# Step sizes of a Mamba-2 layer as fp32 products on four groups of 32 output columns, C0 beside B0 in the opening of a hybrid decoder step

## The chip, the cores and the metric

The kernel is one launch on one core of a Trainium2 chip. Its metric is the time of one execution on the device in microseconds (us). A core has five engines that run their own instruction streams in order: TensorE (PE, matrix products into PSUM; its weight loads are listed as PEld), VectorE (DVE), ScalarE (ACT), GpSimd (POOL) and SyncE (SP), which here only issues transfers. SBUF is the working memory with 128 partitions; PSUM takes what PE writes, in eight banks of 512 fp32 columns.

## The reference, cut to what matters

One decoder layer for 1024 prompt tokens and 8 sample tokens that share all weights, so 1032 tokens in all. Every mixer reads the same RMSNorm(x) through one input projection `w_in`; one of them is a state space model whose step sizes `dt` come from 32 of its columns:

```python
sc_b, sc_c, sc_x, z, xbc, dt_raw, q, gates = jnp.split(xn @ w_in, splits, axis=-1)
xbc_c, ssm_conv_new = causal_depthwise_conv(xbc, ssm_hist, ssm_conv_w)
xbc_c = jax.nn.silu(xbc_c + ssm_conv_b)
xs, bm, cm = jnp.split(xbc_c, [SSM_D_INNER, SSM_D_INNER + SSM_GROUPS * SSM_STATE], axis=-1)
dt = jax.nn.softplus(dt_raw.astype(jnp.float32) + ssm_dt_bias.astype(jnp.float32))
a = -jnp.exp(ssm_a_log.astype(jnp.float32))
y_ssd, ssm_new = ssd_fn(xs, dt, a, bm, cm, ssm_s0)
```

`xbc` has 24 blocks of 128 columns: 16 of x, four of B, four of C. B0 and C0 are the first block of each (blocks 16 and 20). `z` has 16 blocks. A cross-attention reads keys and values made from RMSNorm of a memory of 256 tokens. All of it is fp32.

## The kernel before, in words

**Products.** Activations lie transposed: 8 tiles of 128 model columns by 1032 tokens. A large product is made of three passes in a faster format (fp32r): an operand is split into a high part (a cast by ScalarE) and the rest (a subtraction by VectorE), and high x high, high x low and low x high are summed in PSUM. A plain block of 128 output columns (`gemm`, L184) is 8 k-tiles x 3 passes x 3 thirds of 344 tokens = 72 matmuls; its PSUM tile has three banks, and two such tiles exist ("mm"). Two further banks ("sm", two buffers of one bank) serve all small products and transposes. Every weight block goes through `weights` (L146): a load of 512 KB, the cast, the subtraction; of raw, high and low tiles there are three each.

**The opening (L390 to L517).** x is loaded, normalised and transposed in three thirds. `to_xn` (L452) makes, for a third and a k-tile, `xw` (the normalised x in fp32, L458), its high part (L459) and its low part (L460), and writes the raw transpose to DRAM for later (L456, out of three buffers). `first_products` (L488) multiplies a third and k-tile by two weight blocks at once: dt's (128 columns of `w_in` of which the first 32 are dt) and B0's. The products of a third follow while the next third is made. Both "mm" tiles are taken by ps_dt and ps_B0. Behind the opening come the transposes of the histories for the convolutions (ps_h, L530), and ps_dt is emptied with its bias into dtr (L551).

**Behind the opening (L1151 to L1229).** `xbc_tile` (L735) takes B0 from PSUM (L739), convolves it (`conv`, L647: a scaled copy on ScalarE, three passes of 1.2 us on VectorE, small ones for the 8 sample tokens) and applies SiLU; two copies of a few columns on GpSimd keep the convolution's tail (L725) and B for the sample tokens (L732). C0 is a `gemm` of its own, then the same. `make_forms` (L1133) makes the sums and differences of the blocks of xn that the Strassen products need: with b11, b12, b21, b22 the quarters of xn (k-tiles 0 to 3 and 4 to 7, first and second half of the tokens), T1 = b12 - b11, T3 = b22 - b12, nT2 = T1 - b22 and T4, each in four k-tiles, in place in xw where that is possible, and each split into high and low. z0 and z1 are plain blocks (`z_step`, L757). From then on blocks go in pairs through `strassen` (L290), seven products of 24 matmuls (Z2 is the pair of z blocks 2 and 3; its weights are A, S, T and D, its forms B11, T1, nT2, B21, T3, B22, T4).

**Small pieces.** `pend` is a queue of small pieces of work which `tick` issues one at a time between the matmuls of a large product: three ticks in a plain block, three in a pair. Here it holds, in this order, the softplus of dt (`dt_softplus`, L562: nine transposes of dtr, then some twenty passes on VectorE), its running sums (`dt_sums`), their rows to DRAM (`dt_rows`) and what the sample tokens need (`dt_sample`: four copies into exs, L633, and 33 transposes into ps_ex). Then `flush` empties the queue, and the memory follows: its load, its norm (`mem_rms`, L1177), its transposes (`mem_t`) and 16 half blocks of keys and values (`kv_block`). The buffers of the dt work (pool "pdt") end at L1158, and the memory's (pool "pm", L1160) take their place.

**What sets the order.** A planner at compile time orders each engine's instructions: among those that it reckons ready, program order goes first; it also gives tiles their buffers. So work far behind can fill a gap, and an instruction whose buffer is still taken waits, with all that was put behind it on its engine. The buffers that matter most here are the five of the pool "ev" (4 KB a partition): x tiles, histories, dtr, the u and acc of a convolution, the raw differences for T3, z results, memory tiles and the sums of Strassen weights all rotate through them.

## Time and profile before

| what | value |
|---|---|
| median of 3 runs | 2502.28 us (2502.19 to 2504.86) |
| the profiled execution | 2503.04 us |
| its span in the profile | 2501.3 us |
| busy share of PE, DVE, ACT, POOL | 98%, 61%, 42%, 5% |
| granted clock of PE, mean | 0.995 |

The page is one execution taken by the hardware's profiler; times in it count from the span's start. Part 1 is the busy time of each engine, part 2 the span in 40 slices, part 4 the chain of work that ended last, followed back from the last instruction. In the order of time a row is: start, duration of one or length of the merged group, engine, line, operation, output <- inputs, shapes, xcount, and in brackets how long the engine was idle before it and what ended that. A matmul's row ends later than the next one starts, since they are pipelined; what a matmul takes is read from start to start. An fp32 matmul shows as two instructions. "128*32" is 128 rows by 32 columns of loaded weights.

### The profile page before, as it was taken

Reading aid. Unit: us, or ns where it says so; the run is one execution under the profiler, and the core shown is the slowest. Engines: PE = TensorE matmul, PEld = TensorE weight load, DVE = VectorE, ACT = ScalarE, POOL = GpSimd, SP = SyncE. Lnnn points to the kernel's source line nnn. Section 1 sums busy time; section 2 is a strip of 40 time slices with the busy share of each in tenths; the row PEclk is TensorE's granted clock in tenths of the full one; section 3 lists DMA queues with packets and bytes.
Section 4 is the critical chain, followed back from the end, with each engine's and each line's share of the span. In section 5 each row is a group of like instructions: output and inputs, shape, how many; then the busy total and the mean of one; then the engine's idle time right before and its main releaser. Section 6 shows DMA issues by size and latency. Waiting matters only on the chain.

```text
span 2501.3 us, 44971 instructions
## 1 busy us (share of the span) xinstructions
PE 2461.6 (98%) x18714; PEld 2399.9 (96%) x18714; DVE 1519.3 (61%) x2590; ACT 1047.0 (42%) x1688; POOL 135.3 (5%) x163
## 2 busy tenths in 40 slices
PE   7999999999999999999999999999999999999998
PEld 6999999999999998999989998999999999999998
DVE  6754586777677773766866662655775545453325
ACT  6554455454545534556545441223433333341212
POOL 0300000000000000321120000000000000000000
PEclk9999999999999999999999999999999999999999
DMA  6344434344344455668867686945442222282211
GB/s 202 110 150 154 128 104 143 110 140 126 99 136 136 127 160 190 192 211 266 276 199 277 218 303 218 327 144 178 140 151 95 85 68 85 86 274 89 68 34 69
DMA packets 348331, 392.08 MB, mean 157 GB/s; under 512 B 15334, under 2 KB 285782, under 8 KB 348119
## 3 DMA queue, kind: packets, MB, share of 16 engines
q1 hardware_dynamic: 327678, 331.50, 42.1%
q10 hardware_dynamic: 20449, 57.71, 6.1%
q8 instruction: 147, 2.41, 0.4%
q14 instruction: 57, 0.47, 0.1%
HBM read 280.40 MB, written 108.98 MB: 156 GB/s over the span
## 4 chain that ended last, share of the span: by engine, by line
PE 92%; DVE 2%; DMA 2%; ACT 2%; issue 1%; SPq 0%; ACTq 0%; DVEq 0%; POOL 0%
PE po L203 14%; PE pd L203 9%; PE ps_q L203 4%; PE pm L1701 4%; PE py L941 1%; PE pss L959 1%; PE ps_g L203 1%; PE po L933 1%; PE ps_z L203 1%; PE u20m L248 1%; PE u6m L248 1%; PE g20m L248 1%; PE u18m L248 1%; PE g18m L248 1%; PE u16m L248 1%
## 5 line engine op out<-in xcount | busy, mean ns | idle before, releaser
L1843 DVE TENSOR_TENSOR x<-pd,x 128x1032 f32<-128x1032 f32 x24 | 29.6, 1231 | 131.2 <-PE pd L203 131.2
L888 ACT ACTIVATE r<-r,acum 128x128 f32<-128x128 f32 x256 | 78.8, 391 | 5.3 <-DMA r<-ac_d 4.9
L659 DVE SCALAR_TENSOR_TENSOR ax<-u,prm,ax 128x1024 f32<-128x1024 f32 x44 | 56.3, 1280 | 0.1
L920 POOL TENSOR_TENSOR xdd<-xdt,decst 128x512 f32<-128x512 f32 x32 | 38.0, 1189 | 296.5 <-DVE xdt L916 296.5
L829 ACT ACTIVATE st<-st,es 128x128 f32<-128x128 f32 x128 | 41.9, 394 | 22.4 <-DMA st<-in_state_ssm_dram 20.5
L914 DVE TENSOR_TENSOR r<-r,cbm 128x1024 f32<-128x1024 f32 x32 | 39.0, 1218 | 9.5 <-ACT r L889 9.2
L1348 DVE TENSOR_TENSOR yr<-po,yr 128x1032 f32<-128x1032 f32 x8 | 9.9, 1232 | 53.8 <-PE po L203 53.8
L913 ACT COPY bT<-bp 128x128 f32<-128x128 f32 x32 | 8.5, 265 | 79.9 <-DVE cbm L911 79.9
L831 DVE SCALAR_TENSOR_TENSOR st<-sr,dts,st 128x128 f32<-128x128 f32 x128 | 40.2, 346 | 0.4
L941 PE MATMUL py<-r,xdt 128*64 128x128 f32 x512 | 35.9, 284 | 4.4 <-issue 4.4
L937 DVE TENSOR_TENSOR yt<-po,ea 128x512 f32<-128x512 f32 x28 | 19.3, 689 | 32.5 <-PE po L933 29.7
L941 PEld LDWEIGHTS py<-r,xdt 128*64 128x64 f32 x512 | 28.1, 139 | 8.7 <-issue 5.3
L950 DVE SCALAR_TENSOR_TENSOR x<-x,dpar,yt 128x128 f32<-128x128 f32 x128 | 36.2, 345 | 0.2
L835 DVE SCALAR_TENSOR_TENSOR sr<-st,sr 128x128 f32<-128x128 f32 x128 | 35.4, 286 | 1.1
L972 POOL TENSOR_TENSOR s<-s,cdec 128x512 f32<-128x512 f32 x28 | 35.1, 1253 | 0.5 <-DVE s L965 0.4
L889 ACT ACTIVATE r<-r 128x1024 f32<-128x1024 f32 x32 | 33.9, 1060 | 0.6
L959 PE MATMUL pss<-xdd,bT 128*128 128x512 f32 x64 | 33.5, 605 | 0.0
L1708 DVE TENSOR_TENSOR x<-pm,xT 128x516 f32<-128x516 f32 x16 | 11.1, 696 | 36.4 <-PE pm L1701 36.3
L933 PE MATMUL po<-bc,s 128*128 128x128 f32 x224 | 29.5, 275 | 0.0
L933 PEld LDWEIGHTS po<-bc,s 128*128 128x128 f32 x224 | 28.4, 191 | 0.0
L1630 DVE TENSOR_TENSOR gt<-po,gt 128x1032 f32<-128x1032 f32 x8 | 9.9, 1232 | 30.6 <-PE po L203 28.8
L662 DVE SCALAR_TENSOR_TENSOR ax<-u,prm,ax 128x1032 f32<-128x1032 f32 x22 | 28.3, 1286 | 0.0
(9105 smaller groups left out, 8947.7 us busy)
## 6 DMA issues: line engine op xcount, KB each, us to landing
r<-ac_d SPq DMA_DIRECT2D x32, 512.0 KB
gt<-gt_d SPq DMA_DIRECT2D x24, 516.0 KB
xs_d<-ax ACTq DMA_DIRECT2D x22, 516.0 KB
hr<-h_d SPq DMA_DIRECT2D x22, 516.0 KB
gt_d<-G ACTq DMA_DIRECT2D x20, 516.0 KB
x<-xs_d SPq DMA_DIRECT2D x16, 516.0 KB
zs<-zs_d SPq DMA_DIRECT2D x16, 516.0 KB
yb_d<-x SPq DMA_DIRECT2D x16, 516.0 KB
```

Of the source, the lines that this page charges most:

```text
L203: PE.matmul(ps[:, n, :CW], wt[:, ks], x[:, n * CW : (n + 1) * CW], start=(k == 0 and i == 0), stop=(k == nk - 1 and i == 2),)
L248: PE.matmul(ps[:, n, :HC], wt[:, ks], x[:, n * HC : (n + 1) * HC], start=(start and kt == 0 and i == 0), stop=(kt == 3 and i == 2), skip_g ...
L659: V.scalar_tensor_tensor(acc[:, :T], u[:, j : j + T], w[j], acc[:, :T], op0=ALU.mult, op1=ALU.add)
L829: S.activation(st[:, i], st[:, i], AF.Copy, scale=es[:, g * 4 + i, b : b + 1])
L831: V.scalar_tensor_tensor(st[:, i], rb, dts[:, g * 4 + i, b : b + 1], st[:, i], op0=ALU.mult, op1=ALU.add)
L888: S.activation(r[:, j, :], r[:, j, :], AF.Relu, scale=-1.0, bias=acum[:, c, h : h + 1])
L914: V.tensor_tensor(r, r, bc(cbm.unsqueeze(1), [P, HPG, P]), op=ALU.mult)
L920: G.tensor_tensor(b3(xdd, HPG), b3(xdt, HPG), bc(decst[:, c, hs].unsqueeze(2), [P, HPG, 64]), op=ALU.mult)
L933: PE.matmul(po[:, t * P : (t + 1) * P], state["s"][:, t * P : (t + 1) * P], bcg[1][:, cs], start=True, stop=True,)
L941: PE.matmul(py[hp : hp + 64, (h // 2) * P : (h // 2 + 1) * P], xdt[:, h * 64 : (h + 1) * 64], r[:, (h % 2) * 4 + h // 2, :], start=True, s ...
L959: PE.matmul(pss, bT, xdd, start=True, stop=True)
L1701: PE.matmul(ps[:, n, :HC], wt[:, ks], x[:, half * HT + n * HC : half * HT + (n + 1) * HC], start=(k == 0 and i == 0), stop=(k == KD - 1 an ...
```

## The change

- The two blocks of `first_products` are B0 and C0. Both "mm" tiles now hold these.
- dt's weight block is loaded but not split. After the products of a third, `step_sizes` multiplies it in plain fp32: 8 matmuls of 344 tokens, one per k-tile, with 32 loaded columns; k-tile k writes to the 32 partitions of group k mod 4, so that four groups hold a quarter of the sum each (two k-tiles). The result takes one "sm" buffer and goes by ScalarE, with the bias in the first group and 0 in the others, into dtr, which now has 128 partitions.
- `fold` (a sum of the four 32 x 32 blocks of the identity's rows) adds the four quarters: the nine transposes of dtr become nine fp32 products of dtr with fold, 32 columns each.
- xw is read by these products until the end of each third.
- C0's own `gemm` behind the opening is gone; `xbc_tile` takes B0 and C0 from PSUM one after the other, and both `make_forms` follow.
- The pieces of dt are ticked in z0 and z1. `mem_rms` writes its squares into PSUM (four activations of 512 columns and an addition in place of two of 1024) and keeps its sums in another pool, and it is ticked in z1; `flush`, the end of "pdt" and the start of "pm" come behind z1.

```diff
--- before.py
+++ after.py
@@ -393,7 +393,7 @@
     h_xc = cn.tile([P, 24, 24], F32, tag="h_xc", name="h_xc")
     xn = [(act_tile("ah", f"xnh{k}"), act_tile("al", f"xnl{k}")) for k in range(KD)]
     xw = [act_tile(("ah", "al")[k % 2], f"xw{k}", F32) for k in range(KD)]
-    ps_dt, ps_b0 = mm_ps("ps_dt"), mm_ps("ps_B0")
+    ps_b0, ps_c0 = mm_ps("ps_B0"), mm_ps("ps_C0")
 
     with tc.tile_pool(name="p0", bufs=1) as p0:
         xin = []
@@ -438,12 +438,17 @@
         def par(key, i):
             return prm[:, PC[key] + i : PC[key] + i + 1]
 
-        w_dt = weights(wblock(w_in, C_DT), "wdt")
         w_b0 = weights(wblock(w_in, C_XBC + 16 * P), "wB0")
+        w_c0 = weights(wblock(w_in, C_XBC + 20 * P), "wC0")
+        w_dt = load_raw(wblock(w_in, C_DT), "wdt")
+        bias = cn.tile([P, 1], F32, tag="bias", name="bias")
+        V.memset(bias, 0.0)
+        SY.dma_start(bias[:HEADS], a["ssm_dt_bias"].rearrange("l h -> h l"))
         st = p0.tile([P, 9], F32, tag="st", name="st")
         rst = p0.tile([P, 9], F32, tag="rst", name="rst")
         V.memset(st, 1.0)
         rbc = p0.tile([P, TT], F32, tag="rbc", name="rbc")
+        dtr = []
         xs_sb = p0.tile([NS, D], F32, tag="xs", name="xs_sb")
         for i in range(3, NCK):
             load_x(i)
@@ -489,10 +494,24 @@
             cw = slice(g3 * CW, (g3 + 1) * CW)
             ah, al = xn[k]
             ks = slice(k * P, (k + 1) * P)
-            for ps, (wh, wl) in ((ps_dt, w_dt), (ps_b0, w_b0)):
+            for ps, (wh, wl) in ((ps_b0, w_b0), (ps_c0, w_c0)):
                 PE.matmul(ps[:, g3, :CW], wh[:, ks], ah[:, cw], start=(k == 0), stop=False)
                 PE.matmul(ps[:, g3, :CW], wh[:, ks], al[:, cw], start=False, stop=False)
                 PE.matmul(ps[:, g3, :CW], wl[:, ks], ah[:, cw], start=False, stop=(k == KD - 1))
+
+        def step_sizes(g3):
+
+            cw = slice(g3 * CW, (g3 + 1) * CW)
+            ps = sm_ps(f"ps_dt{g3}")
+            for k in range(KD):
+                q = k % 4
+                PE.matmul(
+                    ps[q * HEADS : (q + 1) * HEADS, :CW], w_dt[:, k * P : k * P + HEADS], xw[k][:, cw],
+                    start=(k < 4), stop=(k >= 4),
+                )
+            if g3 == 0:
+                dtr.append(ev_tile("dtr"))
+            S.activation(dtr[0][:, cw], ps[:, :CW], AF.Identity, bias=bias)
 
 
         for i in range(3):
@@ -511,8 +530,11 @@
                     first_products(g3 - 1, k)
                 if g3 < 2 and k == 5:
                     root_of(g3 + 1)
+            if g3:
+                step_sizes(g3 - 1)
         for k in range(KD):
             first_products(2, k)
+        step_sizes(2)
 
         SY.dma_start(r_d, rbc[0:1, :])
 
@@ -545,10 +567,8 @@
 
     dt_stack = ExitStack()
     pd_ = dt_stack.enter_context(tc.tile_pool(name="pdt", bufs=1))
-    bias = pd_.tile([HEADS, 1], F32, tag="bias", name="bias")
-    SY.dma_start(bias, a["ssm_dt_bias"].rearrange("l h -> h l"))
-    dtr = ev_tile("dtr", (HEADS, TT))
-    V.tensor_scalar(t3(dtr), flat(ps_dt)[:HEADS], bias, None, op0=ALU.add)
+    fold = pd_.tile([P, HEADS], F32, tag="fold", name="fold")
+    V.tensor_reduce(fold, ident.rearrange("p (q h) -> p h q", q=4), axis=AX.X, op=ALU.add)
     W = 9 * HEADS
 
     def small(name):
@@ -562,8 +582,10 @@
     def dt_softplus():
         ps = sm_ps("ps_dtT")
         for c in range(NCK):
-            PE.transpose(ps[:, c * HEADS : (c + 1) * HEADS], dtr[:, c * P : (c + 1) * P], ident[:HEADS, :HEADS])
-        PE.transpose(ps[:NS, 256:288], dtr[:, T:TT], ident[:HEADS, :HEADS])
+            PE.matmul(
+                ps[:, c * HEADS : (c + 1) * HEADS], dtr[0][:, c * P : (c + 1) * P], fold, start=True, stop=True
+            )
+        PE.matmul(ps[:NS, 256:288], dtr[0][:, T:TT], fold, start=True, stop=True)
         V.memset(x0[:, 256:], 0.0)
         V.tensor_copy(x0[:, :256], ps[:, :256])
         V.tensor_copy(x0[:NS, 256:], ps[:NS, 256:288])
@@ -732,9 +754,7 @@
             G.tensor_copy(bcs[:, ct % 4, :, ct // 20], acc[:, T:TT])
         S.dma_start(xs_d[ct], acc[:, :TT])
 
-    def xbc_tile(ct, name, ps=None, w=None):
-        if ps is None:
-            ps = gemm(w, xn, "ps_" + name)
+    def xbc_tile(ct, name, ps):
         u = ev_tile("u" + name)
         S.copy(t3(u, 3), flat(ps))
         xbc_conv(ct, u, name)
@@ -1148,24 +1168,16 @@
             V.scalar_tensor_tensor(b12, b12, par("mix", kt), rb[:, HS[1]], op0=ALU.mult, op1=ALU.mult)
         return ts
 
-    w_c0 = weights(wblock(w_in, C_XBC + 20 * P), "wC0")
     xbc_tile(16, "B0", ps_b0)
+    xbc_tile(20, "C0", ps_c0)
     make_forms(0)
-    xbc_tile(20, "C0", w=w_c0)
     make_forms(2)
     z_step(0)
-    flush()
-    dt_stack.close()
-    mem_stack = ExitStack()
-    pm = mem_stack.enter_context(tc.tile_pool(name="pm", bufs=1))
-
-
-    mst = pm.tile([P, 2], F32, tag="mst", name="mst")
-    mrs = pm.tile([P, 2], F32, tag="mrs", name="mrs")
-    memT = [
-        (pm.tile([P, KD, P], F32R, tag=f"mh{m}", name=f"memh{m}"), pm.tile([P, KD, P], F32R, tag=f"ml{m}", name=f"meml{m}"))
-        for m in range(2)
-    ]
+
+
+    mst = cn.tile([P, 4], F32, tag="mst", name="mst")
+    mrs = cn.tile([P, 2], F32, tag="mrs", name="mrs")
+    memT = []
     mem_sb = []
 
     def mem_load():
@@ -1176,9 +1188,13 @@
 
     def mem_rms():
         for m in range(2):
-            junk = memT[m][0].rearrange("p k c -> p (k c)")
-            S.activation(junk, mem_sb[m], AF.Square, accum_out=mst[:, m : m + 1])
-        rsqrt(pm, mrs, mst, D, [P, 2], "m")
+            for half in range(2):
+                S.activation(
+                    sm_ps(f"junk{m}{half}"), mem_sb[m][:, half * 512 : (half + 1) * 512], AF.Square,
+                    accum_out=mst[:, 2 * half + m : 2 * half + m + 1],
+                )
+        V.tensor_add(mst[:, :2], mst[:, :2], mst[:, 2:])
+        rsqrt(cn, mrs, mst[:, :2], D, [P, 2], "m")
         for m in range(2):
             V.tensor_scalar(mem_sb[m], mem_sb[m], mrs[:, m : m + 1], None, op0=ALU.mult)
 
@@ -1223,10 +1239,16 @@
         S.dma_start(scr[:, :, c].rearrange("m p c -> p m c"), t)
 
     mem_load()
-    pend.extend([None, mem_rms, None])
+    pend.append(mem_rms)
+    z_step(1)
+    flush()
+    dt_stack.close()
+    mem_stack = ExitStack()
+    pm = mem_stack.enter_context(tc.tile_pool(name="pm", bufs=1))
+    for m in range(2):
+        memT.append(tuple(pm.tile([P, KD, P], F32R, tag=f"m{i}{m}", name=f"mem{i}{m}") for i in "hl"))
     pend.extend(lambda m=m: [mem_t(m, half) for half in range(2)] for m in range(2))
     pend.extend(lambda j=j, q=q: kv_block(j, q) for j in range(8) for q in range(2))
-    z_step(1)
 
     def plain3():
         for kt in range(4):
```

## The prediction

> **What bounds the kernel now.** I read the page first (busy shares and the chain of waits), then the busy time by stage, then the opening engine by engine.
>
> ```profile
> span 2501.3 us, 44971 instructions
> PE 2461.6 (98%) x18714; PEld 2399.9 (96%) x18714; DVE 1519.3 (61%) x2590; ACT 1047.0 (42%) x1688; POOL 135.3 (5%) x163
> PE 92%; DVE 2%; DMA 2%; ACT 2%; issue 1%; SPq 0%; ACTq 0%; DVEq 0%; POOL 0%
> ```
>
> TensorE (PE) is busy 98% of the span and is 92% of the chain that ended last. So a microsecond taken off PE counts only where PE then has something else ready, and the stage that changes has to be looked at by itself. The busy time by stage, up to the start of the memory keys (first number behind the comma: length of the stretch):
>
> ```profile
> core 0: us, PE busy (x) PEld busy (x) DVE busy (x) ACT busy (x) POOL busy (x), PEclk, DMA share, GB/s
> 57.40:61.71 4.31, 2.20 (x33) 2.04 (x33) 3.56 (x7) 4.28 (x7) 0.10 (x1) 1.00 0.14 24
> 61.71:75.52 13.81, 13.81 (x81) 13.53 (x82) 13.81 (x27) 7.71 (x10) 13.13 (x3) 0.88 0.20 71
> 75.52:100.35 24.83, 24.32 (x155) 23.62 (x153) 22.53 (x41) 16.24 (x21) 10.82 (x2) 1.00 0.31 109
> ...
> 105.94:125.62 19.68, 19.68 (x161) 18.88 (x160) 12.05 (x20) 9.32 (x13) 0.00 (x0) 0.94 0.35 92
> 125.62:140.84 15.22, 14.19 (x114) 13.74 (x113) 11.17 (x27) 14.56 (x37) 0.00 (x0) 0.97 0.39 139
> ```
>
> The stretches are: the seam behind the opening; C0's product; z0 and z1; Z2 from the first product of its form T1 on; Z4 up to the memory keys. The reader is to see two things. PE is full from 61.71 on. And VectorE (DVE) is as full: all of 13.81 us under C0, 22.53 of 24.83 us under z0 and z1. Only from 105.94 on has it room (12.05 of 19.68). The two engines arrive at Z2 together. The seam and C0 in order of time on PE:
>
> ```profile
> 57.31 2.29 PE L530 MATMUL ps_h<-ident,hist 24*128 24x24 f32 x32
> ...
> 61.71 1.23 PE L203 MATMUL ps_C<-xnh,wC0h 128*128 128x344 f32 x3 [2.11 <-DVE dtr L551]
> ...
> 65.23 0.63 PE L203 MATMUL ps_C<-xnl,wC0h 128*128 128x344 f32 x3
> ...
> 66.27 0.68 PE L565 MATMUL ps_dtT<-ident,dtr 32*128 32x32 f32 x8
> 66.91 0.74 PE L203 MATMUL ps_C<-xnh,wC0h 128*128 128x344 f32 x3
> ...
> 75.52 0.64 PE L203 MATMUL ps_z<-xnh,wz0h 128*128 128x344 f32 x3
> 75.99 0.63 PE L203 MATMUL ps_z<-xnl,wz0h 128*128 128x344 f32 x3
> ```
>
> C0 starts 2.11 us late because its PSUM buffer is the one that VectorE is still emptying into dtr. Its first 12 products (four rows of three) need 65.23 - 61.71 = 3.52 us; at z0's pace (three in 0.47 us, the last two rows) they would need 1.88, so a slow clock costs 1.6 us (granted 0.88 in the third stretch). C0 ends at 75.52.
>
> **The change, part by part.**
>
> *PE, products.* In the opening dt's 72 products of 344 columns give way to 72 of C0: equal. Behind it C0's own 72 go: 72 x 0.157 = 11.3 us less. The 24 fp32 products come on top. The trace has two neighbours: fp32 products on 32 columns in four groups (the cached values), and one fp32 product over the full array (ac).
>
> ```profile
> 1499.41 1.07 PE L1492 MATMUL pso<-vc,pTs 128*32 128x256 f32 x16
> 1500.41 0.74 PE L203 MATMUL po<-b03h,wo21h 128*128 128x344 f32 x3
> 96.94 0.59 PE L592 MATMUL ps_ac<-da,tri 128*128 128x256 f32 x2
> 97.37 0.59 PE L593 MATMUL ps_ac<-da,ones 128*128 128x256 f32 x2
> ```
>
> One fp32 product is two instructions. Over the full array, 256 columns take 97.37 - 96.94 = 0.43 us. Eight on four groups, 256 columns each, take 1500.41 - 1499.41 = 1.00 us, where one after the other they would take 3.44. So the groups overlap. Scaled by 344/256: 1.34 us for a third of the tokens, 4.0 for three. The upper bound is no overlap at all: 24 x 0.43 x 344/256 = 13.9 us. The lower is 24 products over four groups without any start cost, 3.5 us. I take 4.0, because that row has the same form (eight in a row, four groups, fp32 on both sides).
>
> The Trainium skill, "TensorEngine Tiling (Array Packing)", section "Theoretical Speedup", gives up to 4x for 32 columns, and its "Key Properties" say that a change of tiling mode drains the array. By the 4x the three thirds would be an estimated 3.5 us; the trace agrees with most of it (3.44 to 1.00 is 3.4x), and 1.00 less 2 x 0.43 leaves at most 0.14 us for entering and leaving the mode, so the drain does not change the sum.
>
> *The fold.* Nine transposes (66.27 to 66.91, 0.64 us) become nine fp32 products against fold, 18 instructions that each load 128 columns. Nearest row, fp32 with 128 loaded columns and a single moving one:
>
> ```profile
> 1056.21 2.06 PE L1060 MATMUL psny<-ones,sqa 128*128 128x1 f32 x18
> 1058.14 0.72 PE L203 MATMUL ps_q<-xnl,wq4h 128*128 128x344 f32 x3
> ```
>
> 18 in 1.93 us: +1.3 us. Bounds: 0.64 (as the transposes, +0) and 3.9 (18 at 0.21, half of the 0.43 above).
>
> *The seam.* With C0's product in the opening, z0 is the next large product. Its PSUM buffer is B0's, which ScalarE empties in 1.00 us (row below) while PE does the last third of the step sizes (1.34) and the history transposes (2.29). So the 2.1 us wait goes, and I let the 1.6 us of slow clock go with it, since PE no longer pauses there; if it stays slow, that is 1.6 back.
>
> Sum on PE: -11.3 + 4.0 + 1.3 - 2.1 - 1.6 = **-9.7 us**, if nothing new holds PE.
>
> *VectorE and ScalarE.* These rows of the groups and of the order of time carry it:
>
> ```profile
> L551 DVE TENSOR_SCALAR dtr<-ps_dt,bias 32x1032 f32<-32x1032 f32 x1 | 1.3, 1271 | 0.0
> L153 DVE TENSOR_TENSOR wz0l<-wz0r,wz0h 128x1024 fp32r<-128x1024 f32 x1 | 1.2, 1215 | 0.0
> 45.10 0.69 DVE L1127 TENSOR_TENSOR xw<-xw 128x516 f32<-128x516 f32 x1
> ...
> 51.60 0.69 DVE L1127 TENSOR_TENSOR xw<-xw 128x516 f32<-128x516 f32 x1
> 61.28 1.00 ACT L739 COPY uB<-ps_B 128x1032 f32<-128x1032 f32 x1
> 101.29 0.67 DVE L316 TENSOR_TENSOR Z2sa<-Z2sa,Z2r 128x512 f32<-128x512 f32 x1
> 105.41 1.23 DVE L236 TENSOR_TENSOR Z2Sl<-Z2sa,Z2Sh 128x1024 fp32r<-128x1024 f32 x1 [1.59 <-ACT Z2Sh L235]
> 117.33 0.67 DVE L633 COPY exs<-dtT 8x1024 f32<-8x1024 f32 x1
> 122.97 1.06 ACT L1180 ACTIVATE memh<-mem 128x1024 fp32r<-128x1024 f32 x1 [2.69 <-PE ps_ex L638]
> 128.52 1.42 DVE L1183 TENSOR_SCALAR mem<-mem,mrs 128x1024 f32<-128x1024 f32 x2
> ```
>
> dtr leaves VectorE (-1.27); ScalarE takes it in three pieces with room to spare (7.71 of 13.81 busy). One split of weights goes (wdt is used raw); as a third pair of split buffers is now free during the opening, z0's split can run there: -1.2 behind it. The reduction into fold is one small pass (0.2, as the other 128-column passes). In return the four differences b12 - b11 (45.10 to 51.60, 0.6 each) overwrite xw, which the step sizes now read: they must wait for the products of their third and move from the opening to its end, into the idle 2 us that VectorE has there (3.56 of 4.31 in the seam is mostly other work, so I count them as +1 of their 2.4). mem_rms no longer writes into the memory tiles, so it need not wait for the step-size buffers (2.69 us at 122.97, released by the last ps_ex): its 1.4 us of VectorE and some small steps, and perhaps dt_sample's 2.7 (four copies like that at 117.33), can come ahead of Z2.
>
> VectorE's backlog ahead of Z2 ended at 101.97 before. Now: 101.97 - 1.27 - 1.2 + 0.2 + 1 = 100.7, or 104.8 with memory and sample work put ahead. Z2's second factor needs a cast and a subtraction more (1.0 + 1.2): **T1's product can start between 102.9 and 107, against 105.94 before.** PE would be there at 105.94 - 9.7 = 96.2. So most of PE's gain turns into a wait for VectorE. I take 103.5, nearer the lower end, since the squares and the sample's copies hang on transfers that land late: 2.4 us gained there. What was done ahead need not be done again: of PE's hold-ups between 105.94 and 140.84 (idle 15.22 - 14.19 = 1.0 us, clock 0.94 of 19.68 us and 0.97 of 15.22 us, together 1.6) I take 2 of the 2.6. But PE's new wait of up to 7 us is longer than the 2.11 us that cost 1.6 us of slow clock at 61.71; products without a form (A's with B11 and B21) break it up, so I take half, 0.8 lost, with 0 and 1.6 as bounds. Together -2.4 - 2.0 + 0.8 = **-3.6 us**.
>
> The Trainium skill, "TensorE: Matmul & The Clock Gate", section "HAM oscillation — how this bites in real kernels", says that a gap of over some 3.4 us brings the slow clock back. The row at 61.71 shows it after 2.11 us of idleness behind 2.29 us of small transposes. By the rule the full 1.6 us would be lost and the sum would be an estimated -2.8 us.
>
> *Queues.* The third weight block stands ahead of the five x loads on SP's queue, and the tiles' write-back waits behind those:
>
> ```profile
> 7.75 0.58 SPq L124 DMA_DIRECT2D wB0r<-in_w_in_dram  x1
> 8.38 3.06 SPq L403 DMA_DIRECT2D x<-in_x_prompt_dram  x5
> GB/s 0 151 418 423 66 73 317 317 383 404 412 412 372 117 254 127 127 6 277 34 285 37 282 158 279 246 235 319 319 108 172 110 136 225 269 95 0 7 4 84
> 20.55 1.00 ACT L455 COPY xt<-ps_xt 128x384 f32<-128x384 f32 x2 [0.69 <-DMA xT_d<-xt]
> ```
>
> ScalarE waits there for the write-back (xT_d) until 20.55. The last row is what all transfers moved in the first 62 us, in slices of 1.55 us; 512 KB at its best slices of some 420 GB/s is 1.3 us more, at the mean of about 200 twice that. It is made up by the split of C0 that leaves the middle of the opening, so I count 0, bound +2.6. bias, 0.1 KB, likewise. mem_rms's two squares of 1.06 become four of 512 columns on ScalarE, which waits there anyway; mst and mrs only change pool. Order: step_sizes takes one of two small PSUM buffers that the transposes of x rotate through; bound three times an evacuation, +1.5 us, hidden if PE lags there as it does.
>
> **Rivals.**
>
> *A. VectorE does not bind* and PE keeps its gain: 2502.3 - 9.7 = 2492.6; with up to 2 us of small new waits I say 2493.5. For it: PE could fill the wait with sums that are ready. Against: the stretches above, 36.3 of 38.6 us busy.
>
> *B. GpSimd's small copies hold the evacuation buffers.* There are five ("ev"). B0 and C0 now stand together: two u, two acc, and a raw difference fill them, and the next to ask (the second raw difference, then z0's result) waits until a copy of 8 or 11 columns on GpSimd is done:
>
> ```profile
> 62.34 9.50 POOL L725 COPY tail_xc<-uB 128x11 f32<-128x11 f32 x1 [4.15 <-ACT uB L739]
> ...
> 76.80 0.23 POOL L725 COPY tail_xc<-uC 128x11 f32<-128x11 f32 x1 [1.33 <-ACT uC L739]
> 86.72 10.60 POOL L732 COPY bcs<-aC 128x8 f32<-128x8 f32 x1 [9.69 <-ACT aC L728]
> 97.34 0.34 SPq L1174 DMA_DIRECT2D mem<-in_mem_prompt_dram  x1
> ```
>
> The same copy takes 0.23 us at 76.80, where VectorE is idle, and 9.50 or 10.60 where it is full; SP's load of mem went out at 97.34, when the last one let go. If z0 or the raw difference waits out one such copy, that is up to 10.6 us less the forecast's 3.6: 2509.3, **slower**. It decides from a hold of over 5 us on; against it stands that VectorE itself waiting opens the gap in which the copy ends.
>
> The Trainium skill, "SBUF — State Buffer", section "SBUF: two separate sides", calls the port pair of VectorE and GpSimd an exclusive lock that the loser waits out; the 9.50 and 0.23 agree, and by it nothing bounds the hold while VectorE runs without a gap.
>
> *C. The groups do not overlap* with 344 moving columns: 13.9 instead of 4.0 puts PE at Z2 at 96.2 + 9.9 = 106, where it stood: 2501, with the little that is gained behind it. Against: the 1.00 us row.
>
> *D. The change does less than it says*: the planner fills the wait otherwise, or later stages move by as much. 2502.
>
> **How the numbers follow.** The profiled execution took 2503.04 us, 1.74 around its span; the median is 0.76 below it. The sum moves the median: 2502.3 - 3.6 = 2498.7. Chances: forecast 0.47, A 0.24, B 0.17, C 0.04, D 0.08. The forecast's own range is 2495.5 to 2501.5 (T1's product at 102 to 105, 0 to 2.6 us gained behind it). For 8 in 10 I go from 2491.5 (A with its best) to 2506 (two thirds of B). 0.2% is 5.0 us, about what a measurement of this kernel tells from none: the border is 2497.3, inside the forecast's own range; I put 0.16 of its 0.47 below it. Faster: 0.16 + 0.23 of A = 0.39. Slower: 0.16 of B and 0.02 of C and D = 0.18. Same: the remaining 0.43.
>
> **What would show it.** The step sizes: eight fp32 products on 128*32 in 1.2 to 1.5 us per third; 4.6 speaks for C. The seam: z0 directly behind the history transposes, without 2.1 us of idle PE. The wait: PE idle ahead of Z2S's products, released by VectorE; without it, A. GpSimd: a copy of over 5 us whose end releases a tile that PE or VectorE waits for, B. mem_rms on ScalarE ahead of Z2's end, and no wait on ps_ex there. I am wrong if PE reaches Z4 (125.62 before) earlier by less than 1 us or by more than 8, or if stages behind 141 move by over 2 us of their own.

## The result, and the profile after

The changed kernel took **2516.21 us** (median of 4 runs, 2513.40 to 2519.30), the kernel before 2502.24 (2500.27 to 2504.86) beside it: a ratio of 1.0052, 95% interval 1.0040 to 1.0064, so 14 us **slower**. The forecast was 2498.7. The profiled run of the changed kernel is the longest of its four, 2519.30 us; 3.1 us of what its trace shows at the end are above the median.

The page's first lines:

```profile
span 2517.6 us, 44946 instructions
...
PE 2464.4 (98%) x18699; PEld 2397.8 (95%) x18699; DVE 1519.2 (60%) x2591; ACT 1048.2 (42%) x1694; POOL 124.6 (5%) x163
...
PE 88%; DMA 4%; DVE 3%; ACT 2%; issue 1%; SPq 0%; ACTq 0%; POOL 0%; DVEq 0%
```

PE has 2.8 us more to do than before (2461.6), though 72 products of 0.157 us gave way to 24 others; its share of the chain that ended last fell from 92 to 88%. The busy time by stage, for the stretches that answer to those of before (the seam; z0 and z1; Z2 from T1's product on; Z4 up to the memory keys):

```profile
64.85:69.00 4.15, 3.28 (x43) 3.02 (x39) 3.49 (x9) 4.04 (x6) 0.32 (x3) 0.97 0.64 174
69.00:95.84 26.84, 25.72 (x157) 25.34 (x157) 25.31 (x42) 15.69 (x23) 12.34 (x3) 0.94 0.44 140
100.27:123.83 23.56, 18.51 (x147) 17.39 (x145) 15.85 (x31) 15.37 (x20) 0.00 (x0) 0.99 0.34 98
123.83:154.47 30.64, 23.93 (x169) 21.98 (x169) 16.92 (x37) 17.58 (x47) 0.00 (x0) 0.83 0.17 55
```

z0 starts at 69.00, where C0's product still ran before. Up to there PE gained 6.5 us (75.52 before). But in Z2 PE is idle for 5.05 of 23.56 us, and up to the keys for 6.7 of 30.64, at a clock of 0.83. PE in order of time:

```profile
63.55 1.36 PE L508 MATMUL ps_dt<-xw,wdtr 128*32 128x344 f32 x16
...
67.05 1.17 PE L552 MATMUL ps_h<-ident,hist 24*128 24x24 f32 x16 [0.42 <-ACT dtr L514]
68.18 1.00 PE L585 MATMUL ps_dtT<-fold,dtr 128*128 128x32 f32 x6
69.00 1.21 PE L203 MATMUL ps_z<-xnh,wz0h 128*128 128x344 f32 x3
...
73.34 1.19 PE L585 MATMUL ps_dtT<-fold,dtr 128*128 128x32 f32 x10
...
95.84 0.51 PE L248 MATMUL Z2m<-xnh,Z2Ah 128*128 128x258 f32 x2 [1.12 <-ACT z L780]
...
123.83 0.80 PE L248 MATMUL Z4m<-xnh,Z4Ah 128*128 128x258 f32 x2 [4.23 <-ACT Z4Ah L235]
...
150.21 1.59 PE L1206 MATMUL ps_mt<-ident,mem 128*128 128x128 f32 x8 [2.56 <-DVE meml L1211]
154.47 0.58 PE L1230 MATMUL ps_kv<-wkv00h,memh 128*128 128x256 f32 x1 [2.67 <-DVE meml L1211]
```

From Z2's first product (95.84, 100.35 before) to Z6's (173.5, 161.10 before) both kernels do nearly the same work on PE (after the change also ps_ac and one set of ps_acT, some 1.1 us, which stood ahead of Z2 before). The last row of the same view taken over that stretch, first before, then after (length of the stretch, PE busy, granted clock):

```profile
100.35:161.10 60.75, 59.72 (x485) 0.97 0.46 142
```

```profile
95.84:173.50 77.66, 65.79 (x493) 0.91 0.33 102
```

This is the whole loss: 4.5 us ahead at Z2, 16.9 us lost on the way, 12.4 us behind at Z6 and 12.8 to 14.1 us behind at each pair from there to 765. Idle PE makes 10.8 of it (11.87 against 1.03); the other 6.1 are busy time: that 1.1, and for most of the rest the slower clock (0.91 against 0.97). (A further 4.7 us come at X12 and G12, where ScalarE waits 8.3 us for loads of the sample state, 2.5 before. Whether they belong to the change isn't settled: in the two runs below with the memory part as before the same wait is 4.2 and 7.9 us, and the loss there 1.0 and 2.6.) So what comes late? VectorE's softplus of the step sizes, first before, then after, from the read of ps_dtT to its end in da (after with the pass just ahead):

```profile
71.70 0.41 DVE L568 COPY x<-ps_dtT 128x256 f32<-128x256 f32 x1
...
78.53 0.31 DVE L573 TENSOR_SCALAR z<-u 128x288 f32<-128x288 f32 x1 [1.57 <-ACT u L572]
...
95.60 0.46 DVE L585 SCALAR_TENSOR_TENSOR da<-dtT,abc 128x288 f32<-128x288 f32 x1
```

```profile
89.02 1.29 DVE L355 TENSOR_TENSOR T42al<-xw,T42ah 128x516 fp32r<-128x516 f32 x2
90.23 0.41 DVE L590 COPY x<-ps_dtT 128x256 f32<-128x256 f32 x1
...
97.58 0.31 DVE L595 TENSOR_SCALAR z<-u 128x288 f32<-128x288 f32 x1 [3.23 <-ACT u L594]
...
112.12 0.45 DVE L607 SCALAR_TENSOR_TENSOR da<-dtT,abc 128x288 f32<-128x288 f32 x1
```

ps_dtT lay ready at 74.6, yet VectorE reads it at 90.23: both convolutions and both sets of forms now stand ahead of it in program order, and VectorE works through these first, from 68 us on without a gap (the first row of the second view is one of their passes). Before, C0's product came between the two halves of that work, and the softplus was ticked in it. From there the delay runs on through ScalarE:

```profile
94.76 1.03 ACT L780 ACTIVATE z<-ps_z 128x1032 f32<-128x1032 f32 x1 [4.65 <-PE ps_z L203]
95.81 1.28 ACT L594 ACT_TABLE_LOAD   x1
...
97.10 0.45 ACT L594 ACTIVATE u<-u 128x288 f32<-128x288 f32 x1
...
112.89 1.28 ACT L645 ACT_TABLE_LOAD   x1
...
114.43 1.28 ACT L795 ACT_TABLE_LOAD   x1
...
116.95 1.28 ACT L620 ACT_TABLE_LOAD   x1
...
120.95 1.28 ACT L798 ACT_TABLE_LOAD   x1
...
122.74 1.04 ACT L235 CAST Z4Ah<-Z4r 128x1024 fp32r<-128x1024 f32 x1
...
129.79 0.59 ACT L318 COPY Z<-Z4m 128x516 f32<-128x516 f32 x1 [5.07 <-PE Z4m L248]
130.28 0.61 ACT L1192 ACTIVATE junk<-mem 128x512 f32<-128x512 f32 x1
```

The exponential stands behind z1's SiLU (which waits for PE until 94.76), with a table load of its own. What depends on da then falls into Z2's end, between the SiLUs of Z2: four table loads of 1.28 us within 10 us (before, Z2 has two in all up to that cast, at 100.31 and 114.00), and Z4Ah's cast, which PE waits for (4.23 us), comes at 122.74. The Trainium skill, "ScalarE: Activation LUTs", section "What ACT_TABLE_LOAD costs", gives 1.28 us for the load and 1.38 for a drain with it; the load agrees, and no drain shows here (95.81 to 97.10). The memory comes last: its squares stand on ScalarE behind Z4's first copy, which waits 5.07 us for the late PE, and are done only at 139, so its transposes and its keys slip as well (2.56 and 2.67 us of idle PE, and keys 13.6 us later than the 140.84 of before).

### The profile page after: what moved, and what is told of

Read it like the earlier page. It is cut to its first block, busy times and chain, and to the rows that moved or that the text cites. A ratio compares the mean times of both kernels' runs of the same rounds, so it can differ in the third digit from the quotient of the medians.

```text
span 2517.6 us, 44946 instructions
## 1 busy us (share of the span) xinstructions
PE 2464.4 (98%) x18699; PEld 2397.8 (95%) x18699; DVE 1519.2 (60%) x2591; ACT 1048.2 (42%) x1694; POOL 124.6 (5%) x163
## 4 chain that ended last, share of the span: by engine, by line
PE 88%; DMA 4%; DVE 3%; ACT 2%; issue 1%; SPq 0%; ACTq 0%; POOL 0%; DVEq 0%
PE po L203 12%; PE pd L203 9%; PE pm L1723 4%; PE ps_q L203 3%; PE ps_g L203 2%; PE py L961 1%; PE pss L979 1%; PE ps_z L203 1%; PE Z4m L248 1%; PE po L953 1%; PE C6m L248 1%; PE u20m L248 1%; PE g18m L248 1%; PE g14m L248 1%; PE g20m L248 1%
## 5 line engine op out<-in xcount | busy, mean ns | idle before, releaser
L957 DVE TENSOR_TENSOR yt<-po,ea 128x512 f32<-128x512 f32 x28 | 19.3, 689 | 32.8 <-PE po L953 32.8
L1730 DVE TENSOR_TENSOR x<-pm,xT 128x516 f32<-128x516 f32 x16 | 11.1, 695 | 36.4 <-PE pm L1723 36.3
L678 ACT ACTIVATE ax<-u,prm 128x1024 f32<-128x1024 f32 x22 | 27.4, 1246 | 2.3 <-DVE u L344 1.3
```

## The experiments

All were timed beside the kernel before, whose medians were 2503.5 to 2504.2 there; the times in bold are medians, and the ratios, taken over all runs, differ a little from those of the medians. The theory T at the start: the chain of the step sizes comes late, and all else with it. Rivals: the memory's rearrangement (R1), and the opening (R2).

### The order of the step sizes

```diff
-    pend.extend([None, dt_softplus, dt_sums, dt_rows, dt_sample])
...
-    xbc_tile(20, "C0", ps_c0)
     make_forms(0)
+    dt_softplus()
+    dt_sums()
+    xbc_tile(20, "C0", ps_c0)
     make_forms(2)
+    pend.extend([dt_rows, dt_sample])
     z_step(0)
```

> The kernel after, with the softplus and the sums of the step sizes put in program order between the forms of B0 and the convolution of C0, not behind both forms. Theory T (the chain of the step sizes comes late on VectorE and ScalarE, so its buffers come free late and the memory's transposes and keys with them): ps_dtT is read within 8 us of 74.6 in place of 90.2, da ends near 97 in place of 112.1, the memory's transposes start within 2 us of 130 in place of 145.9, ps_kv before 143 in place of 154.5, and the time falls by 10 to 16 us, to 2497 to 2506. Rival R1 (the memory part, squared into PSUM and flushed only behind z1, is what comes late by itself): the chain is early, ps_kv still starts behind 150, the time stays above 2510. Rival R2 (the opening, with three weight blocks ahead of most of x): ps_kv comes earlier but the time falls by less than 6 us.

**2507.08 us** (its runs spread from 2502.6 to 2512.2, and the profiled one took 2502.7), ratio 1.0012 (1.0004 to 1.0020): 9 us of the 14 are back. ps_dtT is read at 76.19, da starts at 96.03, the memory's transposes start at 127.2 (earlier than expected) and the keys at 137.4, 3.5 us ahead of before. T holds for the larger part (it had said 10 to 16 us); R1 as the cause of that part, and R2, fall. The edit also puts the first forms ahead of C0's convolution, and what that gives by itself isn't separated; the next run moves the softplus alone. But 3.5 us are still lost by the medians, and of PE's waits between 60 and 175 us this is the longest (total, times, longest):

```profile
PE Z4m L248 <- ACT Z4Ah L235: 4.5, 1, 4.5
```

The reverse, in the kernel before: only the queue's filling is moved.

```diff
-    pend.extend([None, dt_softplus, dt_sums, dt_rows, dt_sample])
...
     make_forms(2)
+    pend.extend([None, dt_softplus, dt_sums, dt_rows, dt_sample])
     z_step(0)
```

> The kernel before, and in it only the queue of the step sizes' pieces filled behind the forms of B0 and C0 in place of ahead of the convolutions, so that the softplus runs in z0 and not in C0's gemm. T: the same delay without anything else of the change: the read of ps_dtT near 90 in place of 71.7, ps_kv 8 to 14 us later than 140.8, the time 2510 to 2516. R1 and R2: within 3 us of 2502.

**2507.64 us**, 1.0015 (1.0006 to 1.0024): the delay alone, without the rest of the change, costs 4 us. T had said 8 to 14. The read came at 86.52 and the keys 6.3 us late, half of what they are in the change. The delay is a cause by itself; its price depends on what else is behind.

### The memory part

```diff
     z_step(0)
+    flush()
+    dt_stack.close()
...
-            for half in range(2):
-                S.activation(
-                    sm_ps(f"junk{m}{half}"), mem_sb[m][:, half * 512 : (half + 1) * 512], AF.Square,
...
+            junk = memT[m][0].rearrange("p k c -> p (k c)")
+            S.activation(junk, mem_sb[m], AF.Square, accum_out=mst[:, m : m + 1])
```

> The kernel after, with the memory part as it stood before: the pieces flushed and the step sizes' buffers closed behind z0, the memory's squares written into its own buffer. R1: ps_kv back near 141 to 145 and the time at or under 2506. T: the chain of the step sizes is still behind both forms (ps_dtT read near 90), so ps_kv stays behind 150 and the time within 4 us of 2516.

**2516.26 us**, 1.0053 (1.0041 to 1.0066), ps_dtT read at 90.51, the keys at 153.6: R1 falls. The same edit on top of the early step sizes:

> The kernel after with both undone: the softplus and sums of the step sizes between the forms of B0 and C0's convolution, and the memory part as before. What is left of the change is the arithmetic and the place of C0. Theory T2 (with the step sizes early, the memory's squares are the next to hold ScalarE, in four pieces that wait for the small PSUM buffers, with the cast of Z4's weights queued behind them): the 4.5 us ahead of Z4 go, and the time falls 3 to 5 us below the 2507.1 of the step sizes early alone, to 2502 to 2504, which is no change against before. Rival (the order of the step sizes was all, and what is left is the opening): within 1.5 us of 2507.1.

**2506.82 us**, 1.0008 (0.9999 to 1.0017), the time of the early step sizes alone. T2 named the wrong half of the reason. The wait ahead of Z4 is still there (4.73 us), since not only the four squares into PSUM but also the two squares of before stand ahead of Z4Ah on ScalarE and wait for ps_ex, with a table load for the norm's root behind them:

```profile
124.47 1.06 ACT L1198 ACTIVATE memh<-mem 128x1024 fp32r<-128x1024 f32 x1 [0.55 <-PE ps_ex L660]
...
126.67 1.28 ACT L100 ACT_TABLE_LOAD   x1
...
128.08 1.03 ACT L235 CAST Z4Ah<-Z4r 128x1024 fp32r<-128x1024 f32 x1
```

In the kernel before the same cast went ahead (the square came at 122.97):

```profile
119.22 1.05 ACT L235 CAST Z4Ah<-Z4r 128x1024 fp32r<-128x1024 f32 x1 [1.14 <-PE Z2m L248]
```

The order in which the planner puts them hangs on small differences. The next edit forces it.

### ScalarE's order ahead of Z4

```diff
-    pend.extend([None, mem_rms, None])
+    pend.extend([None] * 6 + [mem_rms, None])
```

> The kernel with the step sizes early and the memory part as before, and the memory's norm queued three ticks further on, in Z4 in place of z1, so that in program order it stands behind the cast of Z4's weights. Theory S (what eats the 2 to 5 us that PE has at Z2 is ScalarE's order: the memory's squares wait for the last of the step sizes' work, ps_ex near 124, and Z4Ah's cast at 128.1 stands behind them): the 4.7 us of idle PE ahead of Z4 go, Z4 starts near 123 to 124 in place of 129.2, and the time falls by 4 to 6 us against 2506.8, to 2501 to 2503. Rival V (VectorE and ps_ex bind there whatever ScalarE's order): PE's wait turns up elsewhere before the keys, the time stays within 1.5 us of 2506.8.

**2500.80 us**, 0.9990 (0.9981 to 0.9999). S holds: the cast goes at 111.29 and PE does not wait ahead of Z4, which starts at 122.3 (129.2 in the kernel without this edit).

```profile
111.29 1.05 ACT L235 CAST Z4Ah<-Z4r 128x1024 fp32r<-128x1024 f32 x1 [1.78 <-PE Z2m L248]
...
123.57 1.07 ACT L1198 ACTIVATE memh<-mem 128x1024 fp32r<-128x1024 f32 x1 [1.21 <-PE ps_ex L660]
```

The control has that same line in the kernel before:

> The kernel before with that same shift of the memory's norm alone, as the control. In it Z4Ah is cast at 119.2, ahead of the squares, and PE waits 0.8 us in all between 106 and 161 for the memory. S: nothing is to be gained, the time within 2 us of before; if the later memory costs something by itself (keys later, wait at their start), up to 3 us more.

**2500.88 us**, 0.9995 (0.9986 to 1.0004): no change that can be measured, as S has it. It also limits what the change's arithmetic is worth. With its two orders mended it stands at 0.9990, the old arithmetic with the same memory queue at 0.9995. The difference between the two, which with its uncertainty of 0.13% reaches from 2 us lost to 4.5 us gained, isn't settled by these runs.

### The arithmetic alone, and the opening

The kernel before with the fp32 step sizes only; C0 keeps its own product.

```diff
-            for ps, (wh, wl) in ((ps_dt, w_dt), (ps_b0, w_b0)):
+            for ps, (wh, wl) in ((ps_b0, w_b0),):
...
+            if g3:
+                step_sizes(g3 - 1)
```

> The kernel before, and in it only the step sizes in fp32 on four groups of 32 columns (with the weight block behind B0's, and the folding products): C0 keeps its own gemm behind the opening, the pieces and the memory keep their places. It prices the arithmetic: 72 matmuls of B0's kind fewer, three times 1.30 us and nine folding products more. The opening ends 10 to 12 us less its 72 products, that is 48 to 51 in place of 57.4 if the pace of the x loads allows it, and not before 53 if it does not. T: the time falls by 3 to 9 us, to 2493 to 2499, as nothing of the chain is moved behind other work. R2 (three blocks of weights in the opening): no third block is there ahead of C0's own, so it falls by as much as the products do. If the opening is bound by its loads, the time stays within 3 us of 2502.

**2510.02 us**, 1.0032 (1.0020 to 1.0044): slower, against every theory. With dt's 72 products out of it, the opening ended not at 48 to 53 but at 64.98, where the history transposes start (57.31 before). The next run puts 72 useless products in their place.

```diff
-    ps_b0 = mm_ps("ps_B0")
+    ps_b0, ps_rep = mm_ps("ps_B0"), mm_ps("ps_rep")
...
-            for ps, (wh, wl) in ((ps_b0, w_b0),):
+            for ps, (wh, wl) in ((ps_rep, w_b0), (ps_b0, w_b0)):
```

> The kernel with only the arithmetic changed (C0 in its own gemm), and in the opening B0's products done twice, the first time into the PSUM tile that dt left free, where nothing reads them: 72 useless matmuls more, 11.3 us of PE at 0.157. Theory K (in the opening PE has nothing to fill its waits with once dt's products are gone, falls to the slow clock, and the transposes of x and with them the whole opening go at that clock): the opening ends no later than the 63.4 of the kernel without them, near 61 to 62, the clock is at 1.00 from 30 on, and the time is equal or up to 3 us less than 2510.0. Rival (the opening of the arithmetic alone is longer for another reason, the fp32 products and the order of its loads): the useless matmuls cost time, 4 us or more.

The stretch from 22 to 57 us, first without, then with the useless products (PE busy, matmuls, clock), then the opening with them from 12 us on, and the longest waits of PE in the first stretch without them:

```profile
22.00:57.00 35.00, 29.67 (x130) 0.71 0.53 163
```

```profile
22.00:57.00 35.00, 29.96 (x181) 1.00 0.56 171
```

```profile
12.00:63.73 51.73, 42.65 (x266) 1.00 0.58 190
```

```profile
PE ps_B L497 <- ACT xnh L463: 2.3, 2, 2.1
PE ps_xt L478 <- DVE xw L462: 2.3, 2, 1.8
```

PE is busy for the same time in both, but without the fill it does 130 matmuls at a mean clock of 0.71, with it 181 at 1.00, and the opening with the useless matmuls in it ends 1.3 us earlier (63.73). So the half of K that speaks of the clock and of the opening is shown. But the clock is the smaller part of what made the opening longer: at 1.00 it still ends 6.4 us later than before (57.31). From 12 us on PE is busy 3.2 us more than before in it (42.65 against 39.49), with the fp32 products, and idle 3.3 us more (9.08 against 5.82); which waits of the chain of x those are was not followed. The Trainium skill, "TensorE: Matmul & The Clock Gate", section "HAM oscillation — how this bites in real kernels", explains slow stretches by waits that outlast a window of some 3.4 us; here none is over 2.1 us, and the clock fell all the same. K's sum for the whole was wrong: **2516.89 us**, 1.0047 (1.0034 to 1.0060). In the first run of the pair the planner had put some of C0's products into the gaps of the opening (from 36.4 us on), and C0 ended at 81.5; the useless ones took that place, and C0 ended at 84.7. So z0 starts 3.2 us later; at Z6 1.9 of these are left, and the rest of the 6.9 us between the two medians appears only behind it and was not traced.

In the change itself the opening has its fill (C0) and loses little of the clock. PE from 12 us to the history transposes, before and after:

```profile
12.00:57.31 45.31, 39.49 (x218) 1.00 0.66 215
```

```profile
12.00:64.85 52.85, 45.12 (x267) 0.97 0.57 186
```

7.5 us longer: 5.6 of busy time, of which the three groups of fp32 products are 3.9 and the slow clock most of the rest, and 1.9 of idle time (7.73 against 5.82). The idle time is ScalarE's first wait on a write-back, and four runs went after it. First, the third weight block loaded behind the x loads, in the change (the first of the two texts) and in the kernel with step sizes and memory back in their places (the second):

```diff
-        w_dt = load_raw(wblock(w_in, C_DT), "wdt")
...
         SY.dma_start(xs_sb, a["x_sample"][:, 0, :])
+        w_dt = load_raw(wblock(w_in, C_DT), "wdt")
```

> The kernel after, and in it only the step sizes' weight block (and the bias) loaded behind the five x blocks. Q: ScalarE's wait on the write-back falls from 2.6 to about 0.7 us, the opening ends about 2 us earlier. But the keys' start is set by the chain of the step sizes on VectorE, which is as long as before; if that chain starts 2 us earlier too, the time falls by 2 us to 2514, if VectorE is full and takes no notice of it, by less than 1.

> As the kernel with step sizes and memory part back, and the step sizes' weight block loaded behind the five x blocks in place of ahead of them. Theory Q (the first write-back of the transposed x waits in the SP queue behind the loads, and holds ScalarE's copy and then PE): the wait of ScalarE on that write-back falls from 2.6 to about 0.7 us, the opening ends 2 us earlier, near 59.5 to 61, PE's clock stays at 1.00 between 22 and 30, and 1 to 2.5 us are left of it at the end: 2500 to 2502. Rival (the opening is then held elsewhere, or the new order of loads delays the third block itself): no change.

**2514.45** (1.0040, 1.0027 to 1.0052) and **2506.19** (1.0008, 0.9999 to 1.0017): no gain that can be measured, and the wait stood as it was (2.7 and 2.6 us). The edit did not test Q, as the block and the bias still went out ahead of the first write-back. The next two do, on the kernel with the memory's norm in Z4:

```diff
+                if g3 == 0 and k == 5:
+                    with tc.issue_after(ins):
+                        w_dt.append(load_raw(wblock(w_in, C_DT), "wdt"))
+                        SY.dma_start(bias[:HEADS], a["ssm_dt_bias"].rearrange("l h -> h l"))
```

> As the kernel with the memory's norm in Z4, and the step sizes' weight block and bias loaded only after five of the first third's transposes are written back, so that no third block stands ahead of the first write-back on SP's queue in whichever order. Q: ScalarE's wait on the write-back falls from 2.31 to under 1 us, PE's idle time up to 30 us falls by about 2 us, its clock is 1.00 between 22 and 30, the opening's last B0 product comes 2 to 3 us earlier than 62.6, and the time falls by 1.5 to 3 us below 2500.8. Rival (the write-back is not what holds the opening, or the block then comes when the first step sizes want it at 46): the opening ends within 1 us of 62.6 and the time stays.

```diff
-        w_dt = load_raw(wblock(w_in, C_DT), "wdt")
+        w_dt = load_raw(w_in[:, C_DT : C_DT + HEADS].rearrange("(k p) c -> p k c", p=P), "wdt")
```

> As the kernel with the memory's norm in Z4, and of the step sizes' weight block only the 32 columns that are used are loaded, 128 KB in place of 512, at the same place ahead of the x loads. If the bytes ahead of the write-back hold the opening, three quarters of the gain of the late load show: wait on the write-back 0.8 to 1.3 us, 1 to 2 us off the time. If it is the number of row pieces (1024 of 128 bytes in place of 1024 of 512) or the place in the queue, the wait stays at 2.0 to 2.6 us and the time at 2500.8.

The SP queue in the change, and ScalarE's wait there and with the block behind the write-back:

```profile
8.48 1.35 SPq L124 DMA_DIRECT2D wdtr<-in_w_in_dram  x1
9.94 1.48 SPq L446 DMA_DIRECT2D bias<-in_ssm_dt_bias_dram  x1
11.46 2.32 SPq L403 DMA_DIRECT2D x<-in_x_prompt_dram  x5
...
15.31 1.63 SPq L461 DMA_DIRECT2D xT_d<-xt  x3
```

```profile
22.44 1.03 ACT L460 COPY xt<-ps_xt 128x384 f32<-128x384 f32 x2 [2.58 <-DMA xT_d<-xt]
```

```profile
20.48 1.02 ACT L459 COPY xt<-ps_xt 128x384 f32<-128x384 f32 x2 [0.55 <-DMA xT_d<-xt]
```

The block and its bias take 2.83 us of issuing on SP, and the first write-back goes out at 15.31 behind them and the x blocks (13.21 before). The place is the cause of the wait: it is 2.31 us in the kernel that both runs start from, 0.55 with block and bias behind the write-back, and still 1.95 with a quarter of the block's bytes at the old place. (The two loads were moved together; their shares aren't separated.) But it is worth little. The opening's last B0 product came 1.2 us earlier (61.35 against 62.59), not the 2 to 3 of Q: the clock is 1.00 from 22 to 30 us (0.79 without the edit), but now 0.77 from 40 to 50 (1.00). PE reached Z2 2.9 us earlier (94.3 against 97.2) and Z4 only 0.8 earlier, and Z6 0.7 later: the two times are **2500.19** (0.9985, 0.9976 to 0.9994) and **2500.53** (0.9984, 0.9975 to 0.9993), against 2500.80, a difference that these runs don't settle. Of the 2.9 us, 2.2 are gone at T1's first product (101.39 against 102.06): PE waits 1.17 us for da there and runs at a clock of 0.76 (1.00). These two are the fastest kernels of the study, and their intervals lie below the kernel before, by 0.6 to 0.7 thousandths at the least.

Last, the step sizes of all thirds at the end of the opening:

```diff
-            if g3:
-                step_sizes(g3 - 1)
...
-        step_sizes(2)
+        for g3 in range(3):
+            step_sizes(g3)
```

> As the kernel with the memory's norm in Z4, and the step sizes of all three thirds done at the end of the opening in place of after each third's products. Theory P (the step sizes of the first two thirds stand in the way of the next third's transposes in PE's order, so ScalarE and VectorE wait 1.3 us twice and the chain of x is that much longer): the opening ends 1 to 2.5 us earlier and the time with it, if PE was not full anyway. Rival (from 45 us on PE is full, the products cost their 4 us wherever they stand; and the differences for the forms now wait for all three thirds): the same time, or 1 to 3 us more, as VectorE's work is moved behind the opening.

**2508.87 us**, 1.0022 (1.0012 to 1.0033): P falls. B0's last product came 4.3 us earlier (58.3), but the step sizes then ran from 59.0 to beyond 65, with PE waiting 2.4 us for ScalarE to empty the small PSUM buffers, and z1's last product came at 101.4 in place of 95.7.

### The price of the grouping

```diff
-                    ps[q * HEADS : (q + 1) * HEADS, :CW], w_dt[:, k * P : k * P + HEADS], xw[k][:, cw],
-                    start=(k < 4), stop=(k >= 4),
+                    ps[:HEADS, :CW], w_dt[:, k * P : k * P + HEADS], xw[k][:, cw],
+                    start=(k == 0), stop=(k == KD - 1),
```

> The kernel after with all eight products of a third on the first group of 32 columns, one sum, and the fold over 32 partitions. It prices the grouping, which the prediction took to be worth 13.9 - 4.0 = 9.9 us. If one fp32 product of 344 columns takes two instructions of 0.29 us in a row (the 0.43 us of the full array's 256 columns, scaled), a third takes 4.6 us in place of 1.30, the opening ends 10 us later and the time is 2524 to 2528. If the first two thirds' products lie beside waits of the opening, only the last third shows in full: 2519 to 2523.

```profile
70.61 4.82 PE L507 MATMUL ps_dt<-xw,wdtr 128*32 128x344 f32 x16
75.36 2.48 PE L551 MATMUL ps_h<-ident,hist 24*128 24x24 f32 x32
```

Eight products on one group take 75.36 - 70.61 = 4.75 us; on four they took 1.30 (63.55 to 64.85 above), 3.7 times less. PE came to Z2 11.3 us later than in the change and to Z4 11.6, but the keys came only 7.5 us later, Z6 6.2, and the time is only 5.4 more: **2521.64 us**, 1.0076 (1.0061 to 1.0090). Half of the delay vanished between Z4 and Z6, where PE does the same 314 matmuls with 2.6 us less of idle time and at a clock of 0.95 in place of 0.87.

## Why the prediction was wrong, point by point

- **fp32 products**, 1.34 us a third: 1.30. Right, with the row it came from. Rival C falls with it; the one-group run shows what it would have been (4.75).
- **The fold**, +1.3 us on PE: 18 instructions in 0.82 + 1.28 us (68.18 to 69.00, 73.34 to 74.62), 2.1 in all against 0.64, so +1.5. Right.
- **The seam**: z0 does follow the history transposes without the 2.1 us wait; but the transposes wait 0.9 us for h_xc and dtr, and the slow clock stayed: z0's first six rows of three take 69.00 to 73.34, 4.34 us, 1.5 more than at 0.47 each. The 1.6 us that I let go is the bound I had named.
- **PE sum** of -9.7 ahead of Z2: -4.5 measured. The queue that I counted at 0 with a bound of 2.6 was 1.9 of idle PE, some 1.7 of slow clock in the opening was in no term, and with the seam's 0.9 and 1.5 that makes 6.0; less the 1.1 of ps_ac and ps_acT that moved behind Z2, 4.9 of the 5.2 that are missing. (The granted clock of 0.88 that the prediction quotes for C0 is that of its second stretch, not the third.)
- **VectorE at Z2**: wrong, and this is the step that failed. I took VectorE's backlog ahead of Z2 to stay as long as it was (T1's product at 102.9 to 107) and even let the memory's and the samples' work come ahead of it, with 2.0 us regained behind. That the pieces are now ticked in z0 and z1 is in the description of the change; I did not follow them from there on VectorE: both convolutions and both forms now stand ahead of them. So VectorE did not hold T1 (its product began at 100.27, ahead of the 102.9 to 107), because the softplus was no longer there: where the queue's filling alone is moved in the kernel before, T1 also comes earlier, at 103.12 in place of 105.94. The softplus was read 18.5 us later, and the term of "2.0 regained" behind T1, up to the keys, had the wrong sign: that stretch took 54.2 us in place of 34.9, 19.3 lost (from Z2's to Z6's first product 16.9). Moving the softplus and the sums back gave 9 of the 14 us.
- **Where the wait moved**: to ScalarE's table loads and casts ahead of Z4 and to the memory's transposes and splits (2.56 and 2.67 us of idle PE), which I had only as a gain ("need not wait for the step-size buffers"). The squares no longer waited for the memory tiles, as said, but stood behind Z4's copy on ScalarE and began at 130.28, later than the 122.97 of before.
- **Rival A**'s sign was seen (no wait of PE for VectorE ahead of Z2S) and its time was not: it had no term for the work that had been put off. **Rival B**: one copy on GpSimd does hold for 11.62 us (bcs<-aC, from 78.73), but the memory's load alone goes out at its end, at 90.38, and PE does not wait for that. The other three copies took 0.19 to 0.53 us (at 67.97, 70.20 and 75.56) though VectorE was busy then too, so a full VectorE alone does not make such a copy long. The 0.18 that the prediction gave to "slower" stood almost all on B, so it is no credit to it. **D** falls with the time.
- The tests in the prediction's last part: Z4 came 1.8 us earlier, inside 1 to 8; but from there to the keys 15.4 us were lost (30.64 against 15.22), and behind 141 X12 and G12 moved by a further 4.7, over the 2 that were named as what would prove it wrong.
- With both orders mended the kernel stands 2.7 us below the kernel before, near the forecast's 3.6; but the control stands 2.6 below with the old arithmetic, so this does not speak for the forecast.

## What to carry to other kernels

When a change takes out a large product, list the small work that was issued between its matmuls and follow it, instruction by instruction, on the engine that runs it: its place in program order moves with the product, behind everything that was programmed after. A gain on PE that arrives at a stage where ScalarE or VectorE has a chain of its own is worth what that chain leaves. And an engine's in-order queue is to be read for what stands behind the one instruction that waits: here one cast behind two squares cost 6.0 us by the medians, 4.5 by the ratios.

## What was not expected of the hardware

- In an opening that other engines pace, PE did 130 matmuls from 22 to 57 us at a mean granted clock of 0.71, with no wait over 2.1 us in that stretch; with useless matmuls added it did 181 at 1.00 in the same busy time, and the opening was 1.3 us shorter.
- Eight fp32 products of 344 columns on four groups of 32 take 1.30 us, on one group 4.75.
- A write-back of 192 KB that was issued behind a third block of 512 KB and the bias on one queue held ScalarE 2.31 us (2.58 in the change), with 128 KB there 1.95, and 0.55 with both loads behind it.
